# A transformer trunk in split float32: operands of a part's last step spread over products, matmuls on zeros in front, the last output tiles by halves

## The chip, the cores and the metric

The kernel runs on one core of a Trainium2 chip. The metric is the device time of one execution in microseconds. TensorE (PE in the profile) multiplies matrices, VectorE (DVE) and ScalarE (ACT) work on tiles in on-chip memory, GpSimd (POOL) and SyncE (SP) mostly issue transfers (DMA). The engines run side by side, each takes its own list of instructions in order, and they wait for each other by semaphores.

## The reference

Two layers on 512 tokens of width 1024, all in float32. Each layer is a half-weighted SwiGLU network (FFN), a mixer, and a second FFN; the inner width of an FFN is 2816.

```python
for layer in range(2):
    x = x + 0.5 * swiglu(rms_norm(x, ...), w_gate, w_up, w_down)
    h = rms_norm(x, mix_norm[layer])
    x = x + (even_mixer if layer % 2 == 0 else odd_mixer)(h, ...)
    x = x + 0.5 * swiglu(rms_norm(x, ...), w_gate, w_up, w_down)
return rms_norm(x, final_norm)

def swiglu(x, w_gate, w_up, w_down):
    return (silu(x @ w_gate) * (x @ w_up)) @ w_down
```

The even mixer is block-sparse attention beside a gated MLP. The odd mixer is differential attention with 8 heads: `a = softmax(q0 k0) - lam * softmax(q1 k1)`, `o = rms_norm(a @ v)` per head, then an output projection.

## The kernel before

**Layout.** `x` lies transposed in on-chip memory, eight tiles `x[k]` of 128 channels x 512 tokens. `LO` and `HI` are the first and last 256 tokens. Rows of 128 features are called f, 22 of them in an FFN; f and f + HF (HF = 11) form a pair.

**Float32 by three products.** Each operand is split into a high part and the rest: `w_hi` by ScalarE (L127), `w_lo` by VectorE (L128), likewise `xh`, `xl` for activations. A product is three matmuls: w_hi by xh, w_hi by xl, w_lo by xh (L177 to L179 with 512 columns, L406 to L408 with 256).

**Seven products.** Most of the FFN uses a scheme of seven products of half size in place of eight (class `Seven`). A step of `Up` makes gate and up for a pair of f and both token halves from seven weight chunks c = 1 to 7; a step of `Down` adds seven products into four tiles of x. Sums of weight quarters are made by adding transfers (GpSimd queue) or by VectorE (L369); sums of activations (L477, L478, L484, L490) and their splits (ScalarE L451, VectorE L452) make the *operands* `H[c, s]`. The results stand in three accumulators `pA`, `pB`, `pD`.

**Parts.** The 11 steps of an FFN fall into `PARTS` = (0,3), (3,6), (6,9), (9,11). Behind each of the first three stand the `Down` steps of that part, woven with the next part's first `Up` products: p1, u5, u2, u6, p5, p6, p3, ... The last step of such a part is `late`: its operands are made in pieces as its results come, in `c11`, `c22`, `c12` and `c21`. There are three such boundaries in each of four FFNs, twelve in all. The last part uses plain products (`down`, tiles `py`).

**What sets the order.** `Stream` holds a list of slots, one for each product. `run` walks over them: `step` first issues what earlier slots left for now with `st.later(n, fn)` (n slots later), then `split_to` splits the weights of up to three slots ahead, then come the loads, then the slot's matmuls. `raws` limits the raw weight buffers that are live; raw, high and low buffers share a pool of 14 (`w4`). A slot after c == 3 is followed by `c12`, one after c == 4 by `c21`. When the program is built, each engine's list is fixed, near this order.

**Odd mixer.** Each head is six functions, put `OD = (3, 4, 6, 7, 9, 10)` slots later: scores `s0` and `s1`, transposes `t` (tile `pt`), values `o`, the norm's column `c` (tile `ocol`, ten small VectorE operations L201 to L212), and `r`, which spreads that column over a bank `pr` by four transposes (L315) and scales `o`. Projections `pq` of other heads lie between.

**Start and end.** ScalarE first runs a Silu on a zero tile `warm`. The gains of the norms are loaded by GpSimd's queue. `first` makes the first gate and up (`pg`, `pu`) as `x[k]` arrives. At the end `last_feed` takes each finished `x[k]`: squares, scaling by the final gain, and behind the last tile the sums over channels (`pc`, L1246), the same ten small operations (`lcol`), the transposes, eight outputs `y` (L1258, L1256) and their transfers.

Of the kernel before, what the change touches and what calls it, by code (L numbers as in the profile page):

```python
# [18 lines left out]
P = 128  # L19
# [13 lines left out]
def trunk_kernel(ctx: ExitStack, tc: tile.TileContext, a, out):  # L33
# [16 lines left out]
    def tmp(name, dt=F32):  # L50
        return t2k("tmp", name, dt)
# [19 lines left out]
    class Stream:  # L71
# [62 lines left out]
        def run(self):  # L134
            for i, (first, end, fn, dense, raws) in enumerate(self.slots):
                self.raws = raws
                if dense:
                    self.step()
                    self.split_to(first + self.SPLIT)
                    self.pre_to(first + self.SPLIT + 1)  # L140
                    self.load(0, first + self.SPLIT + 8)
                else:
                    self.split_to(end)
                    self.load(0, end + (2 if raws == 2 else 8))
                    if i + 1 < len(self.slots):
# [32 lines left out]
        nc.tensor.matmul(o, sh, ml, start=False, stop=False)  # L178
        nc.tensor.matmul(o, sl, mh, start=False, stop=last)  # L179

    warm = tmp("warm")[:, :1]
    nc.vector.memset(warm, 0.0)
    nc.scalar.activation(warm, warm, AF.Silu)

    xs = act.tile([P, KT, T], F32, name="x")
    x = [xs[:, k] for k in range(KT)]
    gains = const.tile([P, 7, KT], F32, name="gains")
    nc.gpsimd.dma_start(gains, a["gains"])
# [154 lines left out]
    class Seven:  # L343
# [66 lines left out]
                    st.later(n, aux)  # L410
            return fn

        def add(self, c):
            st.add([self.item(c)], self.slot(c), dense=True, raws=7)

    def pair(ap):
        return ap.rearrange("p (g t) -> p g t", g=2)
# [5 lines left out]
    def ffn(which, norm, feed):  # L423
# [16 lines left out]
        def seven(s):  # L440
            return s < PARTS[-1][0]

        def hidden(f, s=slice(0, T)):
            g = G[f]
            nc.vector.tensor_mul(g[:, 1, s], g[:, 1, s], g[:, 0, s])

# [20 lines left out]
        def whole_split(f):  # L467
            H[f] = split(G[f][:, 1], "h", "h")
# [34 lines left out]
        class Up(Seven):  # L503
# [14 lines left out]
            def after(self, c):  # L518
                s = self.s
                if c in (1, 6):  # L520
                    return [(1, lambda: self.copied(c))]
                if c == 2:
                    return [(1, self.c11)]
                if c == 7:
                    return [(1, self.c22)]
                if c == 3:
                    if self.late:
                        return [(1, self.c12)]
                    if last(s):
                        return [(1, self.c12), (2, lambda: hidden(s)), (2, lambda: whole_split(s))]  # L530
                    return [(1, self.c12), (2, lambda: hidden(s))] + (
                        [(2, lambda: first_operands(s)), (3, lambda: other_operands(s))] if self.seven
                        else [(3, lambda: whole_split(s))])
                if c == 4:
                    if self.late:
                        return [(1, self.c21)]
                    if last(s):
                        return [(1, self.c21), (1, lambda: hidden(s + HF)), (1, lambda: whole_split(s + HF))]
                    return [(1, self.c21), (2, lambda: hidden(s + HF))] + (
                        [] if self.seven else [(3, lambda: whole_split(s + HF))])  # L540
                return []

# [16 lines left out]
            def quarter_done(self, m, s):  # L559
                g = G[self.s + m * HF]  # L560
                nc.scalar.activation(g[:, 0, s], g[:, 0, s], AF.Silu)
                nc.vector.tensor_mul(g[:, 1, s], g[:, 1, s], g[:, 0, s])

            def c22(self):
                self.copied(7)
# [8 lines left out]
            def c12(self):  # L574
                g = G[self.s]
                nc.vector.tensor_add(g[:, :, HI], self.v[6], pair(self.bank["D"]))
                if self.late:
                    nc.vector.tensor_mul(g[:, :, HI], g[:, :, HI], self.row(HI))
                    self.quarter_done(0, HI)
                    sums_57(self.s)  # L580
                    sum_6(self.s)
                    operand(self.s, 6, sums[self.s][:, LO])
                else:
                    nc.vector.tensor_mul(g, g, norm.row[:, None].to_broadcast([P, 2, T]))
                    nc.scalar.activation(g[:, 0], g[:, 0], AF.Silu)

            def c21(self):
                g = G[self.s + HF]
                nc.vector.scalar_tensor_tensor(g[:, :, LO], pair(self.bank["A"]), -1.0,
                                               self.row(LO), op0=OP.mult, op1=OP.mult)  # L590
# [32 lines left out]
        def down(ds, s0, s1):  # L623
# [19 lines left out]
                            feed(d)  # L643
            return fn


        def product(f, pg, pu):
            t = G[f] = gu_tile()
# [35 lines left out]
                    st.later(1, norm.last_sums)  # L684
            return fn

        def add(items, fn, raws=7):
            st.add(items, fn, dense=True, raws=raws)
# [416 lines left out]
    def odd_mixer(norm, feed):  # L1105
# [21 lines left out]
        def head(h, pair):  # L1127
# [104 lines left out]

    last = norms[6]

    def last_feed(k):
        if k < KT - 1:
            last.square(k)
            nc.scalar.activation(x[k], x[k], AF.Copy, scale=last.gain(k))
            return
        sq = tmp("sq")  # L1240
        nc.scalar.activation(sq, x[k], AF.Square)
        sums = []
        for src in (last.acc, sq):
            pc = bank("pc")
            for t in range(TT):
                nc.tensor.matmul(pc[:, t:t + 1], src[:, t * P:(t + 1) * P], ones1, start=True, stop=True)  # L1246
            sums.append(pc)
        ms = sm.tile([P, TT], F32, name="part_ms")
        nc.vector.tensor_scalar(ms, sums[0][:, :TT], 1.0 / D, EPS, op0=OP.mult, op1=OP.add)
        col = sm.tile([P, TT], F32, name="lcol")  # L1250
        rsqrt(col, sums[1][:, :TT], 1.0 / D, TT, ms)
        pr = bcast_row(col, "R", True)
        for k in range(KT):
            y = t2k(("tmp", "r2")[k % 2], "y")
            if k == KT - 1:
                nc.vector.scalar_tensor_tensor(y, x[k], last.gain(k), pr, op0=OP.mult, op1=OP.mult)  # L1256
            else:
                nc.vector.tensor_mul(y, x[k], pr)  # L1258
            (nc.sync, nc.scalar)[k % 2].dma_start(out[k], y)

    ffn(3, norms[5], last_feed)

# [111 lines left out]
```

## Time and profile before

| | us |
|---|---|
| median of 3 runs | 1854.38 |
| lowest and highest run | 1852.54, 1858.32 |
| the profiled execution's own time | 1857.99 |
| its span, first to last instruction | 1856.3 |
| TensorE busy | 1812.4 (98%) |
| VectorE busy | 1565.8 (84%) |
| ScalarE busy | 957.3 (52%) |

The mean granted TensorE clock of the profiled execution was 0.992 of full speed. In the rows of the profile, a table of waits has: engine, tile and line that waited, what ended it, then us in total, times, longest. A row of the order in time has: start, duration, engine, line, operation, output and inputs, and in brackets the idle time before it with what ended it. The durations of matmuls overlap, so the distance between starts is what one costs.

### The profile page before, as it was taken

To read this page: it belongs to the slowest core of one execution; us is meant where nothing else is said; L and a number is where in the kernel's file an instruction comes from. 1 tells how busy PE (TensorE), PEld (TensorE's weight loads), DVE (VectorE), ACT (ScalarE), POOL (GpSimd) and SP (SyncE) were. 2 spreads that over 40 slices of the span, in tenths; PEclk is the share of its full clock that TensorE was granted. 3 is DMA by queue.
4 is the path that set the end of the run, shared out by engine and by line. 5 is a ranking of instruction groups with operands and counts; after the bars stand their busy time and mean duration, and the time that the engine had idled before them with its cause. 6 is when DMAs were issued, how large, how long until landed. Compare 5 with 4: busy or idle time off the path is not lost. (4 is left out here: it accounts for less than half of the span.)

```text
span 1856.3 us, 32166 instructions
## 1 busy us (share of the span) xinstructions
PE 1812.4 (98%) x12624; PEld 1694.4 (91%) x12624; DVE 1565.8 (84%) x2531; ACT 957.3 (52%) x1523; POOL 236.8 (13%) x231
## 2 busy tenths in 40 slices
PE   8999999999999999999999999999999999999997
PEld 6999999888888999999899999988888889999996
DVE  8888898868968888888988989788989698898986
ACT  6445454533655555454644545455555454454544
POOL 0111111010400111110011111101111001111110
PEclk9999999999999999999999999999999999999998
DMA  7586867412324687865547778742222245868661
GB/s 229 129 219 162 211 158 184 154 68 69 114 93 132 150 220 160 222 154 150 170 115 189 188 192 189 179 152 67 80 87 86 99 139 126 221 160 219 161 171 63
DMA packets 149479, 279.86 MB, mean 151 GB/s; under 512 B 11584, under 2 KB 63440, under 8 KB 149328
## 3 DMA queue, kind: packets, MB, share of 16 engines
q1 hardware_dynamic: 110640, 209.62, 35.1%
q0 software_dynamic: 38112, 67.15, 22.4%
q8 instruction: 99, 1.62, 0.4%
q10 hardware_dynamic: 576, 1.05, 0.1%
q14 instruction: 52, 0.43, 0.1%
HBM read 269.39 MB, written 2.10 MB: 146 GB/s over the span
## 5 line engine op out<-in xcount | busy, mean ns | idle before, releaser
L127 ACT ACTIVATE w_hi<-w_raw 128x1024 fp32r<-128x1024 f32 (+2 forms) x542 | 517.9, 964 | 466.6 <-DVE w_raw L369 144.4
L128 DVE TENSOR_TENSOR w_lo<-w_raw,w_hi 128x1024 fp32r<-128x1024 f32 (+2 forms) x542 | 599.3, 1108 | 152.8 <-ACT w_hi L127 108.2
L359 POOL DMA_DIRECT2D w_raw<-in_gu x72 | 89.1, 1238 | 704.0 <-DMA w_raw<-in_gu 220.8
L406 PE MATMUL pA<-xt,w_hi 128*128 128x256 f32 x576 | 163.5, 284 | 0.0
L407 PE MATMUL pA<-xt,w_hi 128*128 128x256 f32 x576 | 163.3, 283 | 0.0
L408 PE MATMUL pA<-xt,w_lo 128*128 128x256 f32 x576 | 163.2, 283 | 0.0
L406 PE MATMUL pA<-xh,w_hi 128*128 128x256 f32 x576 | 163.0, 283 | 0.0
L406 PE MATMUL pA<-h,w_hi 128*128 128x256 f32 x576 | 163.0, 283 | 0.0
L407 PE MATMUL pA<-h,w_hi 128*128 128x256 f32 x576 | 163.0, 283 | 0.0
L408 PE MATMUL pA<-h,w_lo 128*128 128x256 f32 x576 | 163.0, 283 | 0.0
L408 PE MATMUL pA<-xh,w_lo 128*128 128x256 f32 x576 | 163.0, 283 | 0.0
L407 PE MATMUL pA<-xl,w_hi 128*128 128x256 f32 x576 | 163.0, 283 | 0.0
L406 PEld LDWEIGHTS pA<-xh,w_hi 128*128 128x128 f32 x576 | 110.5, 192 | 0.9 <-ACT v L545 0.8
L406 PEld LDWEIGHTS pA<-xt,w_hi 128*128 128x128 f32 x576 | 111.2, 193 | 0.0
L407 PEld LDWEIGHTS pA<-xt,w_hi 128*128 128x128 f32 x576 | 111.1, 193 | 0.0
L408 PEld LDWEIGHTS pA<-xt,w_lo 128*128 128x128 f32 x576 | 110.9, 193 | 0.0
L407 PEld LDWEIGHTS pA<-xl,w_hi 128*128 128x128 f32 x576 | 110.5, 192 | 0.2
L406 PEld LDWEIGHTS pA<-h,w_hi 128*128 128x128 f32 x576 | 110.6, 192 | 0.0
L407 PEld LDWEIGHTS pA<-h,w_hi 128*128 128x128 f32 x576 | 110.6, 192 | 0.0
L408 PEld LDWEIGHTS pA<-h,w_lo 128*128 128x128 f32 x576 | 110.6, 192 | 0.0
L408 PEld LDWEIGHTS pA<-xh,w_lo 128*128 128x128 f32 x576 | 110.5, 192 | 0.0
L369 DVE TENSOR_TENSOR w_raw<-w_raw 128x1024 f32<-128x1024 f32 (+1 forms) x100 | 109.3, 1093 | 1.5
(279 smaller groups left out, 5390.1 us busy)
## 6 DMA issues: line engine op xcount, KB each, us to landing
w_raw<-in_gu SPq DMA_DIRECT2D x210, 512.0 KB, 4.5
w_raw<-in_gu POOLq DMA_DIRECT2D x92, 512.0 KB, 6.7
w_raw<-in_wd SPq DMA_DIRECT2D x120, 384.0 KB, 3.7
w_raw<-in_wd POOLq DMA_DIRECT2D x48, 384.0 KB, 5.9
w_raw<-in_wd SPq DMA_DIRECT2D x64, 128.0 KB, 2.4
w_raw<-in_oqk SPq DMA_DIRECT2D x16, 512.0 KB, 4.6
ks<-ks SPq DMA_DIRECT2D x24, 256.0 KB, 3.4
w_raw<-in_eqk SPq DMA_DIRECT2D x8, 512.0 KB, 3.3
```

The lines of the kernel that those rows point to most:

```text
L127: nc.scalar.activation(hi, raw, AF.Copy)
L128: nc.vector.tensor_sub(lo, raw, hi.bitcast(F32))
L359: nc.gpsimd.dma_start(dst, src, accum_op=OP.add)
L369: return lambda: nc.vector.tensor_add(r[dst], r[dst], r[other])
L406: nc.tensor.matmul(o, w[0][:, s], t[0], start=new and p + j == 0, stop=False, **go)
L407: nc.tensor.matmul(o, w[0][:, s], t[1], start=False, stop=False, **go)
L408: nc.tensor.matmul(o, w[1][:, s], t[0], start=False, stop=p == self.n - 1, **go)
```

## The change

It has six pieces.

1. In a `late` step the operands that depend on the last two products are no longer made at once. After c == 3: `c12` one slot later, the sums 5 and 7 two later, the sixth operand three later. After c == 4: `c21` one slot later, the last product of gate and up two later, the second operand three, the fourth four.
2. Two float32 matmuls of 128 x 512 zeros (`pw`) stand in front of TensorE's list; they wait for the Silu on `warm`. The gains are loaded by ScalarE's queue, first of all, instead of GpSimd's.
3. In the last FFN the last three output tiles are made by `down_halves`: for all three the first 256 tokens, then the other 256. `last_feed` works by halves; there are two tails, and 16 output transfers of 256 columns instead of 8 of 512.
4. In the first FFN the plain chunks are split before `step` as well (`dense=2`).
5. `raws` is 5 instead of 7 for the last `Up` step and the last `down` products.
6. In the odd mixer `r` comes one slot later for the first seven heads.

```diff
@@ Stream.run
                 if dense:
+                    if dense == 2:
+                        self.split_to(first + self.SPLIT)
                     self.step()
                     self.split_to(first + self.SPLIT)
@@ start
-    warm = tmp("warm")[:, :1]
+    gains = const.tile([P, 7, KT], F32, name="gains")
+    nc.scalar.dma_start(gains, a["gains"])
+    warm = tmp("warm")
     nc.vector.memset(warm, 0.0)
-    nc.scalar.activation(warm, warm, AF.Silu)
+    nc.scalar.activation(warm[:, :1], warm[:, :1], AF.Silu)
+    pw = bank("pw")
+    for n in range(2):
+        nc.tensor.matmul(pw, warm[:, :P], warm, start=True, stop=True)
...
-    gains = const.tile([P, 7, KT], F32, name="gains")
-    nc.gpsimd.dma_start(gains, a["gains"])
@@ Up.after
                 if c == 3:
                     if self.late:
-                        return [(1, self.c12)]
+                        return [(1, self.c12), (2, lambda: sums_57(s)), (3, self.sixth)]
...
                 if c == 4:
                     if self.late:
-                        return [(1, self.c21)]
+                        return [(1, self.c21), (2, lambda: product_of(s + HF, LO)), (3, self.second),
+                                (4, lambda: operand(s, 4, sums[s][:, HI]))]
@@ Up.c12
                 if self.late:
                     nc.vector.tensor_mul(g[:, :, HI], g[:, :, HI], self.row(HI))
                     self.quarter_done(0, HI)
-                    sums_57(self.s)
-                    sum_6(self.s)
-                    operand(self.s, 6, sums[self.s][:, LO])
@@ Up.c21
-                if self.late:
-                    self.quarter_done(1, LO)
-                    operand(self.s, 2, quarter(self.s, 1, LO))
-                    sum_4(self.s)
-                    operand(self.s, 4, sums[self.s][:, HI])
-                else:
-                    nc.scalar.activation(g[:, 0], g[:, 0], AF.Silu)
+                s = LO if self.late else slice(0, T)
+                nc.scalar.activation(g[:, 0, s], g[:, 0, s], AF.Silu)
+
+            def sixth(self):
+                sum_6(self.s)
+                operand(self.s, 6, sums[self.s][:, LO])
+
+            def second(self):
+                operand(self.s, 2, quarter(self.s, 1, LO))
+                sum_4(self.s)
@@ ffn
+        def down_halves(ds, s0, s1):
...
+            def fn(*ws):
+                py = {d: bank("py") for d in ds}
+                for t in (LO, HI):
+                    for d, w in zip(ds, ws):
+                        for f in order:
...
+                            nc.tensor.matmul(py[d][:, t], w[0][:, s], hi[:, t], ...)
+                            nc.tensor.matmul(py[d][:, t], w[0][:, s], lo[:, t], ...)
+                            nc.tensor.matmul(py[d][:, t], w[1][:, s], hi[:, t], ...)
+                        nc.vector.scalar_tensor_tensor(x[d][:, t], py[d][:, t], 0.5, x[d][:, t],
+                                                       op0=OP.mult, op1=OP.add)
+                        feed(d, t)
...
+        early = 2 if which == 0 else 1
...
-                    add([chunk(gu[f, 0])], gate(f))
-                    add([chunk(gu[f, 1])], up(f))
+                    add([chunk(gu[f, 0])], gate(f), dense=early)
+                    add([chunk(gu[f, 1])], up(f), dense=early)
...
-                        steps[s].add(c)
+                        steps[s].add(c, 5 if s == HF - 1 else 7)
...
-            for ds in [ORDER[:2]] + [(d,) for d in ORDER[2:]]:
-                add([chunk(wd[0, d][:, cols], wd[1, d][:, cols]) for d in ds], down(ds, s0, s1))
+            ends = ORDER[5:] if which == 3 else ()
+            for ds in [ORDER[:2]] + [(d,) for d in ORDER[2:] if d not in ends] + [ends] * (which == 3):
+                add([chunk(wd[0, d][:, cols], wd[1, d][:, cols]) for d in ds],
+                    down_halves(ds, s0, s1) if ds == ends else down(ds, s0, s1), 5)
@@ odd mixer, head
-                st.later(n, fn)
+                st.later(n + int(fn is r and h < 7), fn)
@@ last_feed
-    def last_feed(k):
+    def last_feed(k, s=slice(0, T)):
...
-                nc.vector.tensor_mul(y, x[k], pr)
-            (nc.sync, nc.scalar)[k % 2].dma_start(out[k], y)
+                nc.vector.tensor_mul(y, x[k][:, s], pr)
+            (nc.sync, nc.scalar)[k % 2].dma_start(out[k][:, s], y)
```

The line numbers of the changed kernel are some 5 higher in the FFN's helpers (L127 and L128 stay). The instruction lists below have no times; the number at a tile's name tells buffers apart and differs between the two kernels. First VectorE at the second boundary of the first FFN, before: from the product of gate and up behind `c12` (L562), over the sums 5 and 7 (L477, L478), 6 and 4 (L484, L490) and the low parts of operands (L452), to the low part of the chunk that TensorE needs next (L128).

```order
L562 TENSOR_TENSOR gu_1848<-gu_1848 128x256
L369 TENSOR_TENSOR w_raw_1637<-w_raw_1637,w_raw_1528 128x1024
L477 TENSOR_TENSOR h57_1963<-gu_1848 128x256
L478 TENSOR_TENSOR h57_1963<-gu_1889,gu_1848 128x256
L562 TENSOR_TENSOR gu_1889<-gu_1889 128x256
L484 SCALAR_TENSOR_TENSOR h64_1970<-gu_1848,h57_1963 128x256
L619 SCALAR_TENSOR_TENSOR x_70<-pA_2021,x_70 128x2x256
L452 TENSOR_TENSOR h_1967<-h57_1963,h_1966 128x512
L452 TENSOR_TENSOR h_2006<-gu_1889,h_2006 128x256
L490 SCALAR_TENSOR_TENSOR h64_1970<-gu_1889,h64_1970 128x256
L452 TENSOR_TENSOR h_1972<-h64_1970,h_1972 128x256
L128 TENSOR_TENSOR w_lo_2013<-w_raw_1821,w_hi_2012 128x1024
```

The same place of VectorE now, from `c21`'s result (L592). L450 is the former L562, L482 and L483 are the sums 5 and 7, L374 is the former L369, L489 sum 6, L457 the low part of an operand.

```order
L592 SCALAR_TENSOR_TENSOR gu_1892<-pA_1643,R_365 128x2x256
L450 TENSOR_TENSOR gu_1851<-gu_1851 128x256
L128 TENSOR_TENSOR w_lo_2004<-w_raw_1824,w_hi_2003 128x1024
L482 TENSOR_TENSOR h57_1994<-gu_1851 128x256
L483 TENSOR_TENSOR h57_1994<-gu_1892,gu_1851 128x256
L374 TENSOR_TENSOR w_raw_1640<-w_raw_1640,w_raw_1531 128x1024
L457 TENSOR_TENSOR h_1998<-h57_1994,h_1997 128x512
L489 SCALAR_TENSOR_TENSOR h64_2031<-gu_1851,h57_1994 128x256
L450 TENSOR_TENSOR gu_1892<-gu_1892 128x256
L625 SCALAR_TENSOR_TENSOR x_75<-pA_2012,x_75 128x2x256
L457 TENSOR_TENSOR h_2033<-h64_2031,h_2033 128x256
L128 TENSOR_TENSOR w_lo_2039<-w_raw_1640,w_hi_2038 128x1024
```

The low part of that chunk (raw tile 1821 before, 1824 now) moved from behind the operands to the third place, ahead of the sums. On ScalarE at the same place, before (L561 Silu, L451 an operand's high part):

```order
L561 ACTIVATE gu_1848<-gu_1848 128x256
L561 ACTIVATE gu_1889<-gu_1889 128x256
L451 ACTIVATE h_1966<-h57_1963 128x512
L451 ACTIVATE h_2006<-gu_1889 128x256
L127 ACTIVATE w_hi_2012<-w_raw_1821 128x1024
L451 ACTIVATE h_1972<-h64_1970 128x256
```

And now (L567 and L595 Silu, L456 an operand's high part):

```order
L127 ACTIVATE w_hi_2003<-w_raw_1824 128x1024
L456 ACTIVATE h_1929<-gu_1892 128x256
L567 ACTIVATE gu_1851<-gu_1851 128x256
L595 ACTIVATE gu_1892<-gu_1892 128x256
L456 ACTIVATE h_1997<-h57_1994 128x512
L127 ACTIVATE w_hi_2038<-w_raw_1640 128x1024
```

The chunk's high part moved ahead of two Silus and of the operands. On TensorE in the odd mixer, before, where step r of the second head stands: the last `pq` matmuls of one projection, r's transposes, the next head's transposes `pt`, the next scores.

```order
L178 MATMUL pq<-xl,w_hi 128x512
L179 MATMUL pq<-xh,w_lo 128x512
L315 MATMUL pr<-ident,ocol 128x128 x4
L854 MATMUL pt<-ident,e 128x128 x10
L833 MATMUL s<-ks,qs 128x256
```

Where that head's step r stands now: behind one projection more (its last two matmuls begin the list), directly ahead of the products with the values.

```order
L180 MATMUL pq<-xl,w_hi 128x512
L181 MATMUL pq<-xh,w_lo 128x512
L320 MATMUL pr<-ident,ocol 128x128 x4
L179 MATMUL o<-ph,v 128x512
L180 MATMUL o<-pl,v 128x512
```

Step r moved behind `pt`, the scores and one more projection. On VectorE at the end, before: the end of the ten small operations and the eight outputs; the last piece of x (L642) stands ahead of that chain, twelve instructions earlier.

```order
L210 SCALAR_TENSOR_TENSOR rs_20401<-rs_20400 128x4
L211 TENSOR_TENSOR rs_20401<-rs_20401,rs_20399 128x4
L212 SCALAR_TENSOR_TENSOR lcol<-rs_20401,rs_20400 128x4
L1258 TENSOR_TENSOR y<-x,pr 128x512 x7
L1256 SCALAR_TENSOR_TENSOR y<-x,gains,pr 128x512
```

And now: the first half's column `lcol` and its eight outputs, then the last tile's second half.

```order
L671 SCALAR_TENSOR_TENSOR x<-py,x 128x256
L217 SCALAR_TENSOR_TENSOR lcol<-rs_20401,rs_20400 128x2
L1300 TENSOR_TENSOR y<-x,pr 128x256 x7
L1298 SCALAR_TENSOR_TENSOR y<-x,gains,pr 128x256
L1278 TENSOR_TENSOR acc<-acc,sq 128x256
L671 SCALAR_TENSOR_TENSOR x<-py,x 128x256
```

The outputs of the first half moved ahead of the last piece of x.

More of the change, by code (lines that the diff above doesn't have):

```diff
@@ L411, in slot, with add @@
             return fn
-        def add(self, c):
-            st.add([self.item(c)], self.slot(c), dense=True, raws=7)
+        def add(self, c, raws=7):
+            st.add([self.item(c)], self.slot(c), dense=True, raws=raws)
     def pair(ap):
@@ L441, in seven, with product_of @@
             return s < PARTS[-1][0]
-        def hidden(f, s=slice(0, T)):
+        def product_of(f, s=slice(0, T)):
             g = G[f]
@@ L527, in after @@
                     if self.late:
-                        return [(1, self.c12)]
+                        return [(1, self.c12), (2, lambda: sums_57(s)), (3, self.sixth)]
                     if last(s):
-                        return [(1, self.c12), (2, lambda: hidden(s)), (2, lambda: whole_split(s))]
-                    return [(1, self.c12), (2, lambda: hidden(s))] + (
+                        return [(1, self.c12), (2, lambda: product_of(s)), (2, lambda: whole_split(s))]
+                    return [(1, self.c12), (2, lambda: product_of(s))] + (
                         [(2, lambda: first_operands(s)), (3, lambda: other_operands(s))] if self.seven
@@ L535, in after @@
                     if self.late:
-                        return [(1, self.c21)]
+                        return [(1, self.c21), (2, lambda: product_of(s + HF, LO)), (3, self.second),
+                                (4, lambda: operand(s, 4, sums[s][:, HI]))]
                     if last(s):
-                        return [(1, self.c21), (1, lambda: hidden(s + HF)), (1, lambda: whole_split(s + HF))]
-                    return [(1, self.c21), (2, lambda: hidden(s + HF))] + (
+                        return [(1, self.c21), (1, lambda: product_of(s + HF)), (1, lambda: whole_split(s + HF))]
+                    return [(1, self.c21), (2, lambda: product_of(s + HF))] + (
                         [] if self.seven else [(3, lambda: whole_split(s + HF))])
@@ L561, in quarter_done @@
                 nc.scalar.activation(g[:, 0, s], g[:, 0, s], AF.Silu)
-                nc.vector.tensor_mul(g[:, 1, s], g[:, 1, s], g[:, 0, s])
+                product_of(self.s + m * HF, s)
             def c22(self):
@@ L644, in down @@
             return fn
+        def down_halves(ds, s0, s1):
+            n = s1 - s0
+            order = [s for s in range(s0, s1)] + [s + HF for s in range(s0, s1)]
+            def fn(*ws):
+                py = {d: bank("py") for d in ds}
+                go = {"skip_group_check": True}
+                for t in (LO, HI):
+                    for d, w in zip(ds, ws):
+                        for f in order:
+                            i = (f - s0) if f < HF else n + f - HF - s0
+                            s = slice(i * P, (i + 1) * P)
+                            hi, lo = H[f]
+                            nc.tensor.matmul(py[d][:, t], w[0][:, s], hi[:, t],
+                                             start=t == LO and f == order[0], stop=False, **go)
+                            nc.tensor.matmul(py[d][:, t], w[0][:, s], lo[:, t], start=False, stop=False, **go)
+                            nc.tensor.matmul(py[d][:, t], w[1][:, s], hi[:, t], start=False,
+                                             stop=f == order[-1], **go)
+                        nc.vector.scalar_tensor_tensor(x[d][:, t], py[d][:, t], 0.5, x[d][:, t],
+                                                       op0=OP.mult, op1=OP.add)
+                        feed(d, t)
+            return fn
         def product(f, pg, pu):
@@ L685, in up, with add @@
             return fn
-        def add(items, fn, raws=7):
-            st.add(items, fn, dense=True, raws=raws)
+        def add(items, fn, raws=7, dense=1):
+            st.add(items, fn, dense=dense, raws=raws)
+        early = 2 if which == 0 else 1
         add([chunk(gu[0, 0]), chunk(gu[0, 1])], first, 5)
@@ L1233, in trunk_kernel @@
     last = norms[6]
-    def last_feed(k):
+    def last_feed(k, s=slice(0, T)):
+        n = s.stop - s.start
+        sq = tmp("sq")[:, :n]
         if k < KT - 1:
-            last.square(k)
-            nc.scalar.activation(x[k], x[k], AF.Copy, scale=last.gain(k))
+            if last.acc is None:
+                last.acc = t2k("row", "acc")
+                sq = last.acc
+            nc.scalar.activation(sq, x[k][:, s], AF.Square)
+            if sq is not last.acc:
+                nc.vector.tensor_add(last.acc[:, s], last.acc[:, s], sq)
+            nc.scalar.activation(x[k][:, s], x[k][:, s], AF.Copy, scale=last.gain(k))
@@ L1239, in last_feed @@
             return
-        sq = tmp("sq")
-        nc.scalar.activation(sq, x[k], AF.Square)
+        nc.scalar.activation(sq, x[k][:, s], AF.Square)
         sums = []
-        for src in (last.acc, sq):
+        for src in (last.acc[:, s], sq):
             pc = bank("pc")
-            for t in range(TT):
+            for t in range(n // P):
                 nc.tensor.matmul(pc[:, t:t + 1], src[:, t * P:(t + 1) * P], ones1, start=True, stop=True)
-            sums.append(pc)
-        ms = sm.tile([P, TT], F32, name="part_ms")
@@ L1249, in last_feed @@
[L1249 to L1252, printed above, removed]
+            sums.append(pc[:, :n // P])
+        ms = sm.tile([P, n // P], F32, name="part_ms")
+        nc.vector.tensor_scalar(ms, sums[0], 1.0 / D, EPS, op0=OP.mult, op1=OP.add)
+        col = sm.tile([P, n // P], F32, name="lcol")
+        rsqrt(col, sums[1], 1.0 / D, n // P, ms)
@@ L1253, in last_feed @@
+        pr = bank("pr")[:, :n]
+        for t in range(n // P):
+            nc.tensor.transpose(pr[:, t * P:(t + 1) * P], col[:, t:t + 1].to_broadcast([P, P]), ident)
         for k in range(KT):
-            y = t2k(("tmp", "r2")[k % 2], "y")
+            y = t2k(("tmp", "r2")[k % 2], "y")[:, :n]
             if k == KT - 1:
-                nc.vector.scalar_tensor_tensor(y, x[k], last.gain(k), pr, op0=OP.mult, op1=OP.mult)
+                nc.vector.scalar_tensor_tensor(y, x[k][:, s], last.gain(k), pr, op0=OP.mult, op1=OP.mult)
```

## The prediction

> **What bounds the kernel now.** I read the page first (span, busy shares), then the table of waits for TensorE alone, then the granted clock by windows, then the order in time at the places that these two name.
>
> ```profile
> span 1856.3 us, 32166 instructions
> PE 1812.4 (98%) x12624; PEld 1694.4 (91%) x12624; DVE 1565.8 (84%) x2531; ACT 957.3 (52%) x1523; POOL 236.8 (13%) x231
> ```
> ```profile
> PE pB L408 <- DVE w_lo L128: 17.2, 12, 1.6
> PE pg L177 <- ACT xh L227: 5.7, 1, 5.7
> PE pr L315 <- DVE ocol L212: 3.3, 2, 3.1
> PE py L177 <- ACT w_hi L127: 2.3, 4, 0.6
> ```
> TensorE is busy 98% of the span and takes its instructions in order, so the time is its work plus its few waits (columns: us in total, times, longest). The first row comes once in each of the twelve part boundaries, when the step's last operands are made. The second is the start.
>
> ```profile
> 176.60:178.60 2.00, 0.45 (x2) 0.24 (x2) 2.00 (x5) 1.65 (x4) 0.00 (x0) 1.00 0.33 124
> 179.60:182.90 3.30, 3.30 (x18) 3.30 (x17) 1.32 (x2) 0.00 (x0) 1.19 (x1) 0.50 0.19 22
> 183.00:189.00 6.00, 6.00 (x52) 6.00 (x52) 4.37 (x6) 2.85 (x4) 0.10 (x1) 1.00 0.61 143
> 1347.00:1353.70 6.70, 5.96 (x24) 5.67 (x25) 4.76 (x14) 3.96 (x10) 0.00 (x0) 0.50 0.09 34
> 1756.60:1759.90 3.30, 3.30 (x18) 3.30 (x17) 1.52 (x4) 0.00 (x0) 1.20 (x1) 0.50 0.35 35
> ```
> The third number from the right is the granted clock. Within a microsecond after the wait at 176.8 it falls to 0.50 for 3.4 us, then is 1.00 again. It does so after four of the twelve waits (first and last shown), and for 6.8 us in the odd mixer. Inside the kernel I found no low clock that doesn't follow a wait.
>
> **The boundary, the main term.**
>
> ```profile
> 176.77 0.28 PE L407 MATMUL pB<-xl,w_hi 128*128 128x256 f32 x1
> 178.64 0.39 PE L408 MATMUL pB<-xh,w_lo 128*128 128x256 f32 x1 [1.59 <-DVE w_lo L128]
> 178.86 0.28 PE L406 MATMUL pB<-xh,w_hi 128*128 128x256 f32 x1
> 178.98 0.28 PE L407 MATMUL pB<-xl,w_hi 128*128 128x256 f32 x1
> 179.79 0.41 PE L407 MATMUL pB<-xl,w_hi 128*128 128x256 f32 x1
> 180.00 0.41 PE L408 MATMUL pB<-xh,w_lo 128*128 128x256 f32 x1
> ```
> ```profile
> 171.75 0.69 DVE L589 SCALAR_TENSOR_TENSOR gu<-pA,R 128x512 f32<-128x512 f32 x1
> 172.35 0.42 DVE L562 TENSOR_TENSOR gu<-gu 128x256 f32<-128x256 f32 x1
> 172.68 1.22 DVE L369 TENSOR_TENSOR w_raw<-w_raw 128x1024 f32<-128x1024 f32 x1
> 173.82 0.42 DVE L477 TENSOR_TENSOR h<-gu 128x256 f32<-128x256 f32 x1
> ...
> 177.37 1.22 DVE L128 TENSOR_TENSOR w_lo<-w_raw,w_hi 128x1024 fp32r<-128x1024 f32 x1
> 178.50 0.42 DVE L452 TENSOR_TENSOR h<-h,h 128x256 fp32r<-128x256 f32 x1
> ```
> Matmuls of this form follow each other at 0.12 us (178.86 to 178.98), so 176.77 to 178.64 loses 1.87 - 0.12 = 1.75 us. The same at the twelve places gives 1.28 at the first boundary of each FFN and 1.75 at the others: 4 x 1.28 + 8 x 1.75 = 19.1 us (17.2 in the table, which counts from a matmul's end). VectorE is never idle here: the w_lo that TensorE wants at 176.79 stands behind nine instructions on operands and results and one weight sum. Starts are 1.14 us apart for 1024 columns, 0.60 for 512, 0.33 for 256.
>
> The change puts that w_lo directly behind the product of gate and up (VectorE's rows of the order, shown with the change). It then runs at 172.7 to 173.8, three microseconds early. Its w_hi goes ahead of the last two Silus and the operands' high parts on ScalarE, behind which it stood (its two rows of before below), so nothing holds it there.
>
> ```profile
> 174.60 0.63 ACT L451 ACTIVATE h<-h 128x512 fp32r<-128x512 f32 x1 [1.72 <-DVE h L478]
> 175.45 1.04 ACT L127 ACTIVATE w_hi<-w_raw 128x1024 fp32r<-128x1024 f32 x1
> ```
> What is late next? Eight instructions lie between it and the next w_lo: 2 x 0.34 + 1.13 + 0.60 + 2 x 0.34 + 0.60 + 0.34 and its own 1.13, counted from 173.8, make 178.98. TensorE, without the wait, wants it one product of 24 x 0.12 = 2.88 us after 176.79, at 179.67: 0.7 us in hand. The three delayed operands end at about 177.9 (the sixth), 179.3 (the second) and 180.9 (the fourth), by the same spacing; the first product on any of them begins after 184. So I count all twelve waits as gone: **-19.1**, with nothing as the other bound.
>
> In a half-clock stretch the spacing is 0.21 us (179.79 to 180.00): 3.41/0.213 = 16 matmuls, each 0.093 longer, 1.5 us. Four of them: **-6.0**, if the waits cause them (bounds 0 and -6.0). The Trainium skill, "TensorE: Matmul & The Clock Gate", Part 1, says that the clock falls to half after at least one idle window of about 3.4 us. By that rule a wait of 1.6 us should not do it. This trace differs: 1.59 us sufficed in four of twelve cases, so the row decides.
>
> **The last part.** After the last Seven product TensorE waits four times for w_hi of the down weights (fourth row of waits, 2.3 us; start to start, 0.74 each, 2.95 in sum). With the smaller limit on raw buffers and later operands, this ScalarE instruction no longer stands behind a VectorE w_lo. The w_lo itself is then due about 0.15 us after TensorE wants it. **-2.3** (bounds 0 and -2.95).
>
> **The odd mixer.**
>
> ```profile
> 1344.26 0.39 PE L179 MATMUL pq<-xh,w_lo 128*128 128x512 f32 x1
> 1347.74 1.11 PE L315 MATMUL pr<-ident,ocol 128*128 128x128 f32 x4 [3.09 <-DVE ocol L212]
> 1347.53 0.16 DVE L212 SCALAR_TENSOR_TENSOR ocol<-rs,rs 128x4 f32<-128x4 f32 x1
> 1348.89 0.75 DVE L1167 SCALAR_TENSOR_TENSOR o<-o,sg,pr 128x512 f32<-128x512 f32 x1 [1.21 <-PE pr L315]
> ```
> Step r waits 3.48 - 0.23 = 3.25 us for a chain of ten tiny VectorE instructions woven into large ones. One slot later it stands behind a further pq product of 24 x 0.227 = 5.4 us, longer than the wait. VectorE has 1.21 us idle there, so the work that follows has room. Gone with it is the half clock of 6.83 us, in which some 3.1 us are lost. With the two small waits of this kind: **-6.5** (bounds: 0, and -7.0).
>
> **The start.**
>
> ```profile
> 1.35 0.73 POOL L188 DMA_DIRECT2D gains<-in_gains  x1 [0.84 <-POOLq L1362]
> 2.10 0.20 ACT L183 ACTIVATE warm<-warm 128x1 f32<-128x1 f32 x1
> 4.96 0.72 ACT L227 ACTIVATE xh<-x,gains 128x512 fp32r<-128x512 f32 x1 [1.38 <-DMA gains<-in_gains]
> 7.11 0.63 PE L179 MATMUL pg<-xh,w_lo 128*128 128x512 f32 x1
> 478.17 0.38 PE L878 MATMUL o<-pw,vw 128*128 128x128 f32 x2
> 478.39 0.38 PE L854 MATMUL pt<-ident,e 128*128 128x128 f32 x2
> ```
> The gains, issued at 1.35, hold ScalarE until 4.96. At the head of ScalarE's queue they can come up to 1 us sooner, so x's splits run up to 1 us earlier. The zero matmuls have no row of their own. Their nearest is the fp32 one of 128 columns, 0.22 us to the next start at full clock; 512 columns would be 0.87, at half clock 1.74, so two are 3.5 us. From about 2.7 (warm's Silu, after one more DMA issue) they end at 6.2, while real work could begin at 4.8 to 5.7: half a microsecond to 1.4 lost. Against that the clock opens sooner: matmuls of 0.63 us last until 12.3 now and are 0.39 behind. From then on the products follow the splits. I take **-1.2**, bounds +1 and -2.6. The split of first chunks ahead of their sums hardly alters VectorE's order and counts 0, hidden behind products already running.
>
> **The tail.**
>
> ```profile
> 1841.69 0.39 PE L179 MATMUL py<-hh,w_lo 128*128 128x512 f32 x1
> 1846.39 0.16 DVE L212 SCALAR_TENSOR_TENSOR lcol<-rs,rs 128x4 f32<-128x4 f32 x1
> 1847.77 4.27 DVE L1258 TENSOR_TENSOR y<-x,pr 128x512 f32<-128x512 f32 x7 [1.21 <-PE pr L315]
> 1851.96 0.74 DVE L1256 SCALAR_TENSOR_TENSOR y<-x,gains,pr 128x512 f32<-128x512 f32 x1
> ```
> Now: 11.0 us from the last product to the last y's end. By halves, 36 products of 0.227 become 72 of 0.12, +0.5: the last ends near 1842.5. The low half's three tiles are complete 36 x 0.12 = 4.3 us earlier, so its y's can start near 1843.5. But all eight of them, 8 x 0.34 = 2.7 us, stand on VectorE ahead of the high half's last x (see the order), which thus waits until 1846.2 instead of 1842.5. From there its chain (square, sums, ten tiny steps, transposes) takes 5.3 and its y's 2.7: about 1854.0, against 1852.7 now. **+1.3**; bounds +2, and -3.4 if the halves overlap wholly.
>
> **Sum.** -19.1 - 6.0 - 2.3 - 6.5 - 1.2 + 1.3 = -33.8. The profiled execution took 1857.99 us, so 1824.2. Against the median of 1854.38 that is 30 less; that execution lies 3.6 above the median, about what two of its half-clock stretches cost, and these fall away.
>
> **Rivals.**
> 1. The half clock has its own rhythm. All stretches last a multiple of 3.41 us and eight waits of twelve show none; but none lies where TensorE hadn't waited. Then 6.0 + 3.1 stay: 1833. The skill's rule above would give this time.
> 2. The waits move to the next weight. VectorE is 84% busy, and the next w_lo has only 0.7 us in hand by my count. If it comes 1.7 us later than counted, TensorE waits 1 us at each boundary, and 12 come back: 1836. Against it: VectorE's rows there run without a gap, so the count has little room to slip.
> 3. Slower. The sums and operands that are put off arrive after the Down products that read them. Price: three operands at twelve boundaries are 36 places; to lose the gain of 33.8 and 5.6 more, each must be late by 1.1 us. Against it stand over 3 us of slack for each by the count above. It decides only if VectorE runs over 4 us later than counted; then about 1864.
> 4. The edits don't bite: a w_lo moved ahead waits for its own w_hi or its transfer instead. A transfer of such a chunk lands 4.5 us after its issue (row below), longer than the 3 us by which the w_lo comes forward. Then the time stays near the median, 1855.
>
> ```profile
> w_raw<-in_gu SPq DMA_DIRECT2D x210, 512.0 KB, 4.5
> ```
> Against it: the ScalarE rows above show no wait for a transfer ahead of that w_hi.
>
> **Chances.** Forecast 0.62; rival 1 0.10; rival 2 0.18; rival 3 0.03; rival 4 0.05; better than all bounds 0.02. The range must leave out no more than 0.2: down to 1818 (start and tail at their best, 1.4 and 4.7 less), up to 1841, which takes in rivals 1 and 2. A measurement of this kernel tells about 0.3% (5.6 us) from no change. Faster holds forecast, rivals 1 and 2 and the better case, 0.92; no change is rival 4; slower is rival 3.
>
> **What would show it.** Right: no pB row in the waits; clock 1.00 from 13 us to the tail; no 3 us wait for ocol; the w_lo of 172.7 well ahead of its product. Wrong: that row with another tile's name in its place; windows of 0.50 without waits; first real matmul after 6.5; last y less than 11 us after the last product, which would mean that the halves overlap.

## The result, and the profile after

The changed kernel takes 1826.85 us (median of 4 runs, 1825.73 to 1829.13) against 1854.62 (4 runs, 1852.54 to 1858.32): a ratio of 0.985, interval 0.9831 to 0.9868. The profiled execution took 1826.39 us, against 1857.99 before. 1824 was forecast, from 1818 to 1841.

The page's first rows, and TensorE's own rows in the table of waits (us in total, times, longest):

```profile
span 1824.7 us, 32286 instructions
PE 1802.5 (99%) x12664; PEld 1687.0 (92%) x12664; DVE 1566.6 (86%) x2555; ACT 959.4 (53%) x1528; POOL 236.1 (13%) x230
```
```profile
PE pc L1286 <- DVE acc L1278: 3.5, 1, 3.5
PE pw L190 <- ACT warm L187: 2.8, 1, 2.8
PE o L180 <- DVE pl L900: 2.5, 4, 1.0
PE pu L179 <- ACT w_hi L127: 1.3, 1, 1.3
PE py L179 <- DVE pl L900: 0.8, 1, 0.8
PE pA L413 <- DVE w_lo L128: 0.5, 1, 0.5
```
The row of pB for w_lo (17.2 us) is gone, so are py for w_hi in the last part (2.3) and pr for ocol (3.3). New are pc in the tail and, in the odd mixer, `o` for pl, the low part of a transposed tile of scores.

The same boundary, on VectorE and on TensorE:

```profile
169.99 0.42 DVE L450 TENSOR_TENSOR gu<-gu 128x256 f32<-128x256 f32 x1
170.32 1.22 DVE L128 TENSOR_TENSOR w_lo<-w_raw,w_hi 128x1024 fp32r<-128x1024 f32 x1
171.46 0.42 DVE L482 TENSOR_TENSOR h<-gu 128x256 f32<-128x256 f32 x1
...
175.47 1.22 DVE L128 TENSOR_TENSOR w_lo<-w_raw,w_hi 128x1024 fp32r<-128x1024 f32 x1
176.61 0.41 DVE L457 TENSOR_TENSOR h<-gu,h 128x256 fp32r<-128x256 f32 x1
```
```profile
174.16 0.28 PE L412 MATMUL pB<-xl,w_hi 128*128 128x256 f32 x1
174.28 0.28 PE L413 MATMUL pB<-xh,w_lo 128*128 128x256 f32 x1
```
The w_lo ends at 171.5, 2.8 us before TensorE reaches it (174.28); the next ends at 176.6, wanted one product later, at 177.16. TensorE runs through at 0.12 us.

Where the 31.6 us of the span come from, read from the starts of the same matmuls in both traces (us):

| stretch | before | after | gain | forecast |
|---|---|---|---|---|
| start, to the first pD | 58.9 | 57.9 | 1.0 | 1.2 |
| rest of first FFN, to the first pv | 299.7 | 293.5 | 6.2 | 6.9 |
| even mixer, to the first pB | 251.7 | 251.0 | 0.7 | 0 |
| second FFN, to the next first pB | 347.5 | 340.3 | 7.2 | 6.9 |
| third FFN, to the first pq | 293.9 | 286.3 | 7.6 | 6.9 |
| odd mixer, to the first pB | 296.4 | 293.3 | 3.1 | 6.5 |
| fourth FFN without its down part, to the last pD | 267.5 | 260.6 | 6.9 | 6.9 |
| last down part and tail, to the end | 40.6 | 41.8 | -1.2 | - |

The forecast's FFN is 25.1 for boundaries and clock and 2.3 for the last parts, by four. The last two rows cannot be read alone, since the matmuls stand in another order around that pD. Split at the first py of the last part instead, the fourth FFN gains 7.7 and the tail loses 1.9.

### The profile page after: what moved, and what is told of

The parts are those of the page before. It is cut to its first block, busy times and chain, and to the rows that moved or that the text cites. A ratio compares the mean times of both kernels' runs of the same rounds, so it can differ in the third digit from the quotient of the medians.

```text
span 1824.7 us, 32286 instructions
## 1 busy us (share of the span) xinstructions
PE 1802.5 (99%) x12664; PEld 1687.0 (92%) x12664; DVE 1566.6 (86%) x2555; ACT 959.4 (53%) x1528; POOL 236.1 (13%) x230
## 4 chain that ended last, share of the span: by engine, by line
PE 85%; DVE 10%; ACT 2%; DMA 2%; issue 1%; POOL 0%; SPq 0%; DVEq 0%; POOLq 0%; ACTq 0%
PE pA L412 11%; PE pA L413 11%; PE pA L411 11%; PE pD L411 6%; PE pD L413 6%; PE pD L412 5%; PE py L179 3%; PE py L181 3%; PE py L180 3%; PE pB L412 3%; PE pB L411 3%; PE pB L413 3%; PE pu L181 2%; DVE w_lo L128 2%; PE pu L180 2%; PE pu L179 2%
## 5 line engine op out<-in xcount | busy, mean ns | idle before, releaser
L127 ACT ACTIVATE w_hi<-w_raw 128x1024 fp32r<-128x1024 f32 (+2 forms) x542 | 517.8, 964 | 442.8 <-DVE w_raw L374 120.4
L128 DVE TENSOR_TENSOR w_lo<-w_raw,w_hi 128x1024 fp32r<-128x1024 f32 (+2 forms) x542 | 599.5, 1107 | 143.4 <-ACT w_hi L127 98.3
L374 DVE TENSOR_TENSOR w_raw<-w_raw 128x1024 f32<-128x1024 f32 (+1 forms) x100 | 109.2, 1092 | 1.5
```

Of the source, the lines that this page charges most:

```text
L127: nc.scalar.activation(hi, raw, AF.Copy)
L128: nc.vector.tensor_sub(lo, raw, hi.bitcast(F32))
L374: return lambda: nc.vector.tensor_add(r[dst], r[dst], r[other])
```

## The experiments

The kernel before ran beside each set of these: its median was 1856.72, 1855.71 and 1856.37 us in the three. Differences of 1 or 2 us between kernels are therefore read from the traces, between starts of the same matmuls.

**Piece 1 alone.** The kernel before with the new slots for the operands only (`hidden` is the former name of `product_of`).

```diff
                     if self.late:
-                        return [(1, self.c12)]
+                        return [(1, self.c12), (2, lambda: sums_57(s)), (3, self.sixth)]
...
-                        return [(1, self.c21)]
+                        return [(1, self.c21), (2, lambda: hidden(s + HF, LO)), (3, self.second),
+                                (4, lambda: operand(s, 4, sums[s][:, HI]))]
```


> The kernel before with piece 1 alone (operands of late steps spread). Theory: the twelve waits of pB for w_lo go (19.1 us) and with them the four half-clock stretches (6 us), so 25 to 26 us less than a kernel before with four such stretches, about 1829. No pB row in the waits, clock 1.00 after each boundary; the half clock in the odd mixer stays. Rival A (the half clock has its own rhythm): the four stretches stay, about 1835. Rival B (the gain came from the smaller limit on raw buffers or other pieces): about 1854.

1830.37 us against 1856.72 (ratio 0.9861, 0.9846 to 0.9877): 26.4 us. Its waits, and its clock (third number from the right) at two boundaries and in the odd mixer:

```profile
PE pr L315 <- DVE ocol L212: 4.0, 2, 3.7
PE py L177 <- ACT w_hi L127: 2.3, 4, 0.6
PE pu L177 <- ACT w_hi L127: 1.3, 1, 1.3
```
```profile
176.00:180.00 4.00, 4.00 (x35) 4.00 (x35) 4.00 (x7) 0.74 (x3) 1.19 (x1) 1.00 0.37 98
815.00:819.00 4.00, 4.00 (x35) 4.00 (x34) 3.97 (x5) 1.67 (x2) 0.00 (x0) 1.00 0.98 273
1326.70:1333.30 6.60, 5.03 (x22) 4.93 (x23) 4.66 (x15) 3.02 (x7) 0.00 (x0) 0.50 0.18 70
```
No pB row is left and the boundaries run at full clock, while the odd mixer keeps its wait and its half clock. The four waits of py are still there. So piece 1 carries nearly the whole gain, by the mechanism named, and this run's rivals A and B fall.

**Piece 5 undone.** `raws` 7 again in the last Up step and the down products.

```diff
-                        steps[s].add(c, 5 if s == HF - 1 else 7)
+                        steps[s].add(c)
...
-                    down_halves(ds, s0, s1) if ds == ends else down(ds, s0, s1), 5)
+                    down_halves(ds, s0, s1) if ds == ends else down(ds, s0, s1))
```


> The changed kernel without piece 5: the limit on raw buffers is 7 again. Theory: piece 5, not the operands, frees the high part of the first plain down weights, so the four waits of py for w_hi (0.73 us each, present with piece 1 alone) are back: 2.9 us slower than the changed kernel, about 1830. Rival (it comes from the operands and piece 5 together with something else): no such waits, about 1827.

1829.52 us (2 runs; ratio to before 0.9864, 0.9841 to 0.9886), 2.7 more than the changed kernel:

```profile
PE py L179 <- ACT w_hi L127: 2.3, 4, 0.6
```
All four waits are back. The last part's gain is piece 5's, 0.74 a time. The 0.7 us of the even mixer, for which nothing was forecast, goes with piece 5 too: a wait of pv for w_lo of 0.5 us stands there in the three kernels with the limit of 7 (251.7 to 252.3 us for the stretch) and in none with 5 (250.9 to 251.3).

**Piece 6 undone.** Step r at its old slot.

```diff
-                st.later(n + int(fn is r and h < 7), fn)
+                st.later(n, fn)
```


> The changed kernel without piece 6: step r of the odd mixer at its old place. Theory: the wait of 3.2 us for ocol is back, and behind it, with no other wait left in the FFNs, the half clock of 6.8 us; the waits for pl that the changed kernel shows there (1.3, 0.7, 0.9 us) are gone. Net 3 to 4 us slower, about 1830. Rival (the clock has its own rhythm): the wait is back, no half clock; about 1828 or less.

1828.48 us (ratio to before 0.9851, 0.9836 to 0.9867), 1.6 above the changed kernel where 3 to 4 were expected. The wait and a half-clock stretch are back, of one length of 3.41 us instead of two:

```profile
PE pr L320 <- DVE ocol L217: 3.3, 2, 3.0
```
```profile
1323.60:1326.90 3.30, 3.10 (x15) 3.10 (x16) 1.36 (x4) 1.09 (x3) 0.00 (x0) 0.50 0.02 5
```
The odd mixer (first pq to the next pB) takes 295.7 here. With r later it takes 293.3 in the changed kernel and 292.1, 294.2, 294.6 and 294.8 in the four other kernels that differ elsewhere: 293.8 in the mean. So piece 6 is worth 2 us of the 6.5. Nor is the half clock there gone for good: in three of these five (the gains back on GpSimd's queue, no zeros, the tail whole) a stretch of 3.41 us at half clock begins at 1347.7 to 1348.5, behind the waits of `o` for pl, so the single times of this stretch scatter.

**o and c later as well.** The changed kernel with the whole tail, and the odd mixer's o, c and r all one slot later.

```diff
-                st.later(n + int(fn is r and h < 7), fn)
+                st.later(n + int(fn in (o, c, r) and h < 7), fn)
```


> The changed kernel with the tail whole as before, and in the odd mixer not only step r but also o and c one slot later for the first seven heads. Theory: in the changed kernel the products with the values wait for the low part pl (0.9, 0.3, 1.3, 0.7 us), because VectorE is full there; one slot later pl is ready, and 2 to 3 us go: about 1822. Rival (VectorE is the bound of this stage): the waits move to the next tile that VectorE makes, 1824 as with the whole tail alone.

1820.53 us (ratio to before 0.9818, 0.98 to 0.9836); the odd mixer takes 291.0. In the changed kernel, VectorE and TensorE where `o` waits:

```profile
1344.42 1.22 DVE L128 TENSOR_TENSOR w_lo<-w_raw,w_hi 128x1024 fp32r<-128x1024 f32 x1
1345.56 0.69 DVE L826 TENSOR_TENSOR q<-q,sw 128x512 f32<-128x512 f32 x1
1346.16 0.68 DVE L900 TENSOR_TENSOR pl<-pt,ph 128x512 fp32r<-128x512 f32 x1
```
```profile
1345.38 0.48 PE L179 MATMUL o<-ph,v 128*128 128x512 f32 x1
1346.90 0.50 PE L180 MATMUL o<-pl,v 128*128 128x512 f32 x1 [1.04 <-DVE pl L900]
```
TensorE is earlier by the wait that went, and pl stands behind a w_lo on a VectorE without a gap. One slot later the same products find pl ready. In the waits of the kernel with o later no row of `o` is left; the one wait for pl is that of a py at 1417, and pr waits 0.2 us for ocol:

```profile
PE py L179 <- DVE pl L900: 0.8, 1, 0.8
PE pr L320 <- DVE ocol L217: 0.2, 1, 0.2
```
From 296.4 to 291.0 are 5.4 us: most of the 6.5 forecast for r alone, but it needs the neighbours of r moved too. No half clock is left there.

**The tail whole.** The changed kernel without piece 3.

```diff
-            ends = ORDER[5:] if which == 3 else ()
+            ends = ()
...
...
-    def last_feed(k, s=slice(0, T)):
+    def last_feed(k):
```


> The changed kernel without piece 3: the last three output tiles and the final norm whole, as before. Theory: the halves cost 1.9 us, since the first half's outputs stand ahead of the second half's last x on VectorE; so 1.9 us faster than the changed kernel, about 1825, and the last y ends 11 us after the last product again. Rival: the halves gain and something else in the tail costs; then 1829 or more.

1824.31 us (ratio to before 0.9829, 0.9811 to 0.9846), 2.5 less than the changed kernel. In the traces the stretch from the first py of the last part to the end takes 41.79 us here (1781.84 to 1823.63) and 44.05 with the halves (1780.64 to 1824.69): 2.3. Of the changed kernel's tail, VectorE and TensorE:

```profile
1810.12 2.40 DVE L1300 TENSOR_TENSOR y<-x,pr 128x256 f32<-128x256 f32 x7 [0.53 <-PE pr L1294]
1812.45 0.47 DVE L1298 SCALAR_TENSOR_TENSOR y<-x,gains,pr 128x256 f32<-128x256 f32 x1
1812.84 0.41 DVE L1278 TENSOR_TENSOR acc<-acc,sq 128x256 f32<-128x256 f32 x1
1813.17 0.41 DVE L671 SCALAR_TENSOR_TENSOR x<-py,x 128x256 f32<-128x256 f32 x1
...
1821.27 0.47 DVE L1298 SCALAR_TENSOR_TENSOR y<-x,gains,pr 128x256 f32<-128x256 f32 x1
```
```profile
1805.02 0.61 PE L1286 MATMUL pc<-ones,acc 128*128 128x1 f32 x4
1806.52 0.50 PE L1286 MATMUL pc<-ones,sq 128*128 128x1 f32 x4
1809.65 0.43 PE L1294 MATMUL pr<-ident,lcol 128*128 128x128 f32 x2
1814.26 1.01 PE L1286 MATMUL pc<-ones,acc 128*128 128x1 f32 x4 [3.47 <-DVE acc L1278]
```
The first half's eight outputs stand ahead of the last x (1813.17), as forecast. What the forecast had not: the first half's own sums and transposes lie between the products on TensorE (1.0 us). The products of halves come 0.12 apart as forecast, except the five next to these, which take 0.20 to 0.29, 0.6 us more in sum.

**The tail's order.** The same halves, with the first half's outputs put behind the second half's last x and sums (and o, c, r later as above).

```diff
+        if s == HI:
+            last.outputs(range(KT))
         col = sm.tile([P, n // P], F32, name="lcol")
...
+        if s == LO:
+            last.outputs = outputs
+        else:
+            outputs(range(KT))
```


> The changed kernel with o, c and r one slot later and the tail by halves, but the first half's eight outputs put behind the second half's last x and its sums, ahead of its ten small operations. Theory: of the 2.2 us that the halves cost against the whole tail, about 1 us is TensorE work put between the products and 1 us slower products, which stay; the second half's chain starts 2 us sooner, but 1 us of the first half's outputs lies on it: last product to last y 9.5 instead of 11.2 us, about 1821. Rival (the order on VectorE costs nothing, all of it is work): 11 us again, 1822.7.

1820.29 us (5 runs, 1820.03 to 1821.12; ratio to before 0.9808, 0.9794 to 0.9821), the lowest of all, though within 1 us of the two kernels with the whole tail.

```profile
1807.78 0.42 DVE L671 SCALAR_TENSOR_TENSOR x<-py,x 128x256 f32<-128x256 f32 x1 [0.43 <-PE py L669]
1808.19 2.40 DVE L1303 TENSOR_TENSOR y<-x,pr 128x256 f32<-128x256 f32 x7
1810.50 0.48 DVE L1301 SCALAR_TENSOR_TENSOR y<-x,gains,pr 128x256 f32<-128x256 f32 x1
1810.89 0.16 DVE L208 SCALAR_TENSOR_TENSOR rs<-pc,part_ms 128x2 f32<-128x2 f32 x1
1815.99 0.48 DVE L1301 SCALAR_TENSOR_TENSOR y<-x,gains,pr 128x256 f32<-128x256 f32 x1
```
The last product starts at 1807.45, so last product to last y's end takes 9.0 us, against 11.2 in the changed kernel. The order on VectorE alone decides whether the halves lose 2 us or nothing. They win nothing either: from the first py to the last product it still takes 29.8 us, against 27.8 in the kernel with o later and the tail whole, which then needs 11.1 us to the last y's end.

**No zeros.** The changed kernel without the two matmuls on zeros; the gains stay at the head of ScalarE's queue.

```diff
-    pw = bank("pw")
-    for n in range(2):
-        nc.tensor.matmul(pw, warm[:, :P], warm, start=True, stop=True)
```


> The changed kernel without the two matmuls on zeros (the gains still first on ScalarE's queue). Theory: the first real matmul comes at about 5.2 instead of 5.6 us, the clock opens at about 12 instead of 8 us, and the end of the first products is set by the splits of x, so the first boundary comes within 0.5 us of the changed kernel: about 1827. Rival (the zeros make the gain at the start): 1 to 2 us slower, 1828 to 1829, the first pB 1 us later.

1827.25 us (ratio to before 0.9843, 0.9824 to 0.9861), the same. The first real matmul:

```profile
5.10 0.79 PE L179 MATMUL pg<-xh,w_hi 128*128 128x512 f32 x1 [5.10 <-ACT xh L229]
```
It starts at 5.10 instead of 5.59, runs at half clock until 10.5 instead of 8.0 by the clock records, and the first pD comes at 57.75 instead of 57.91.

**The gains back on GpSimd's queue,** with the zeros kept.

```diff
-    nc.scalar.dma_start(gains, a["gains"])
+    nc.gpsimd.dma_start(gains, a["gains"])
```


> The changed kernel with the gains loaded by GpSimd's queue again, behind its first instructions. Theory: the early gains are what is left of the gain at the start; the first split of x waits for them until about 5 us instead of 4.4, and the first pD comes 0.5 us later, at 58.4. Rival (the start is limited elsewhere): 57.9 as in the changed kernel.

One run, 1827.90 us: the first xh waits for the gains, and the first pD comes at 58.81, 0.9 later.

```profile
4.81 0.72 ACT L232 ACTIVATE xh<-x,gains 128x512 fp32r<-128x512 f32 x1 [1.18 <-DMA gains<-in_gains]
```
So the start's gain goes with the gains' queue, not with the zeros. Its size is less sure: with the gains first on ScalarE's queue nine traces have the first pD at 57.75 to 58.18, and the three with GpSimd's queue at 58.26 (piece 1 alone), 58.81 and 58.89.

Piece 4, which the forecast counted as 0, was not undone by itself. Piece 1 alone lacks it and takes 292.8 us from the first pD to the first pv, 0.74 of it a wait of py; the kernels that have it and no late transfer there take 292.0 to 292.2, so nothing of it is seen.

**Made waits.** A transpose, a chain on GpSimd and a second transpose at each boundary (the identity is multiplied by itself, so its values stay).

```diff
+    doses = [2 + 2 * ((5 * i) % 12) for i in range(12)]
+    def stall():
+        pz = bank("pz")
+        nc.tensor.transpose(pz[:, :P], ident, ident)
+        for n in range(doses.pop(0)):
+            nc.gpsimd.tensor_mul(ident, ident, ident)
+        nc.tensor.transpose(pz[:, P:2 * P], ident, ident)
```


> The changed kernel with a made wait at each of the twelve part boundaries: a transpose on TensorE, 2 to 24 small multiplications on GpSimd that must follow it, and a transpose that must follow those; TensorE's list goes on a little in between. The waits should be graded from none to some 4 us. Theory: the half clock follows a wait, if enough of one stretch of 3.41 us is idle (before the change, stretches with 0.38 to 0.43 busy): waits over about 2 us give a half clock of 3.41 us or a multiple, those under 1 us none. Rival A (its own rhythm): no relation between wait and half clock, few or none. Rival B (a whole idle stretch is needed): none under 3.4 us.

1924.75 us (one run). The waits are longer than meant, 0.8 to 11.8 us. The eight of 6.7 us and more and one of 3.25 are followed by half clock; those of 0.8, 2.65 and 3.07 are not, so "over 2 us" is too simple. Windows of 3.4 us (busy time of TensorE in us behind the window's length, clock third from the right):

```profile
641.30:644.70 3.40, 2.19 (x19) 1.99 (x17) 3.40 (x6) 2.08 (x4) 2.50 (x6) 1.00 0.59 210
644.70:648.10 3.40, 1.70 (x14) 1.70 (x15) 3.40 (x6) 0.70 (x3) 1.63 (x4) 1.00 0.00 0
648.10:651.50 3.40, 3.40 (x31) 3.40 (x30) 2.81 (x5) 1.42 (x3) 1.06 (x1) 1.00 0.46 72
1713.10:1716.50 3.40, 1.20 (x11) 0.99 (x9) 3.40 (x6) 1.69 (x2) 3.09 (x5) 1.00 0.66 197
1716.50:1719.90 3.40, 2.50 (x12) 2.51 (x13) 3.32 (x7) 0.83 (x2) 0.96 (x3) 0.50 0.02 5
```
The wait of 3.07 falls across two windows and leaves each at least half busy; that of 3.25 leaves one 1.20 of 3.40, and the next runs at half clock. Rival A (no relation) and rival B (a wholly idle stretch) both fall.

**Without the zeros, with o, c and r later and the tail whole.**

```diff
+            ends = ()
...
+                st.later(n + int(fn in (o, c, r) and h < 7), fn)
```


> The changed kernel with the tail whole, steps o, c and r of the odd mixer one slot later, and without the matmuls on zeros. Theory: the zeros change nothing, so about 1820.5, as with them. Rival (the zeros save about 1 us by opening the clock sooner): 1821.5.

1821.17 us (ratio to before 0.9813, 0.9799 to 0.9826): with the zeros 1820.53, no difference that can be told.

## Why the prediction was right

It forecast 1824.2 for an execution like the profiled one; 1826.4 came. That the sum lies so near is in part luck: the odd mixer fell 3.4 us short, while the FFNs (28.7 to the first py of the last part, 27.4 forecast) and the even mixer (0.7, none forecast) gave 2.0 more. By its own steps:

- **Boundaries, -19.1:** all twelve waits went. The count by row held: 2.8 us early where 3 were forecast, 0.56 us in hand at the next w_lo where 0.7 were. (The 176.79 of the count should be 176.89, 176.77 + 0.12; nothing hangs on it.) Piece 1 alone gave 26.4 with the clock.
- **Half clock, -6.0:** the four stretches of the FFNs went with the waits, in piece 1 alone as well. Rival 1 is out.
- **Last part, -2.3:** right in kind, a little small: four times 0.74 is 2.9, and it is piece 5's.
- **Odd mixer, -6.5:** the step that failed. "VectorE has 1.21 us idle there, so the work that follows has room": it had not. Behind the removed wait VectorE was full, and `o` waited for pl (0.9, 0.3, 1.3, 0.7 us from start to start). 3.1 came in the profiled execution, and about 2 in the mean of five kernels against the one without piece 6. The half clock that was to go with the wait (3.1 of the 6.5) came back, half as long, in three of those five. This is rival 2's mechanism, in a place where the prediction had not looked for it.
- **Start, -1.2:** 1.0, but by the gains alone. The zeros, to which the sum gave a part by an earlier full clock, did nothing: the products there follow the splits.
- **Tail, +1.3:** right in sign and cause, mis-sized: 2.3 against the whole tail. Missing were the first half's sums and transposes in TensorE's own list, 1.0 us, and the 0.6 us that the products next to them lose.
- **Not in the sum:** a wait of TensorE in the first FFN, 1.4 us in three pieces, behind one transfer that came late (ScalarE waited 3.17 us for it at 232). Of the other kernels with the same code there, one shows it at the same place, one at another and most not at all, so it isn't counted to the change.

## What to carry to other kernels

When TensorE waits for the next weight at every boundary, look at what stands ahead of that weight's split in the other engines' lists: here putting off work whose result was needed only microseconds later cost nothing, and took away the half clock that followed such waits. Before counting a wait as gone, read how full the engine is that made it, in the microseconds behind the wait: its next product is wanted earlier by just that wait. A tail cut in two lost 2 us as long as the first half's outputs stood ahead of the second half's first step; with the order turned it drew level with the whole tail, no more.

## What was not expected of the hardware

The half clock keeps a grid of its own. Before, the stretches start at 179.57, 817.86, 1166.02, 1346.92 and 1756.52 in the trace's clock records; the distances to the first are 187, 289, 342 and 462 times 3.4133 us. By these traces what decides is how much of one such window TensorE is idle. Idle is counted here as what the distance between two starts exceeds the usual one of that form, which gives some 0.05 to 0.08 more idle than the busy times in the rows below. In eleven of the twelve traces (behind the start and before the tail), a window at full clock that was idle by 0.48 or less was never followed by half clock, one idle by 0.62 or more always; of eight at 0.50 to 0.51 (1.7 us of wait in one window) six were. Two from the kernel before, side by side: the same wait, the same 1.82 us busy, and only after the first a half clock. The last two rows are from the kernel with the gains back on GpSimd's queue, the twelfth trace.

```profile
176.15:179.56 3.41, 1.82 (x13) 1.42 (x12) 3.41 (x7) 2.75 (x5) 0.00 (x0) 1.00 0.34 127
722.29:725.70 3.41, 1.82 (x14) 1.62 (x14) 3.41 (x7) 2.26 (x4) 0.00 (x0) 1.00 0.19 71
725.75:729.00 3.25, 3.25 (x29) 3.25 (x29) 2.39 (x3) 0.13 (x1) 1.20 (x1) 1.00 0.37 42
1344.47:1347.88 3.41, 2.42 (x15) 1.93 (x14) 3.41 (x5) 1.34 (x4) 0.00 (x0) 1.00 0.92 284
1347.90:1351.20 3.30, 3.05 (x12) 2.57 (x11) 3.25 (x8) 1.03 (x3) 0.00 (x0) 0.50 0.28 108
```
There a window idle by only 0.37 was followed by half clock. It holds eight matmuls of one column (`pc`, 0.95 us), which this count takes as work. If they count as idle, it was idle by 0.59, and all twelve traces agree: 0.48 or less never, 0.50 to 0.51 four of six times, 0.59 or more always. That one-column matmuls count as idle rests on three such windows and was not tried by itself.

So what a wait of 1.75 us costs, 1.75 or about 3.3, depends on where it falls in the grid, which differs from run to run. Of the eight such waits of the kernel before, five lie whole in one window, and half clock followed four of them; three are split over two windows, and it followed none. That fits the scatter of the runs of before: in the three sets, eight with a mean granted clock of 0.995 took 1851.99 to 1856.07 us, eleven with 0.991 or 0.992 took 1855.64 to 1858.10. The Trainium skill, "TensorE: Matmul & The Clock Gate", Part 1, has the free-running window of 3413 ns, which agrees; its condition of at least one idle window doesn't: half an idle window was enough here.
